# First FFN: block 0 projected in two halves of 256 channels, norm sums taken over channels by TensorE

## The chip, the cores and the metric

The kernel runs on one core of one Trainium2 chip. The metric is device time in microseconds (us) of one execution; the time before is the median of 3 runs. Engines are named as in the profile: PE is TensorE, DVE is VectorE, ACT is ScalarE, POOL is GpSimd, SP is SyncE, which issues the DMAs here.

## The reference, cut to what matters

Two layers act on a residual stream `x` of 256 tokens by 2048 channels, float32. Every sub-layer normalizes, scales and shifts; scale, shift and gate come from one vector `c` through large matrices:

```python
sc = jax.nn.silu(c)
shift_m, scale_m, gate_m, shift_f, scale_f, gate_f = jnp.split(sc @ mod_w[i] + mod_b[i], 6, axis=-1)
h = modulate(rmsnorm(x, norm_mix[i]), shift_m, scale_m)
x = x + gate_m[:, None, :] * pool_mixer(h, pool_w[i], pool_scale[i])     # layer 0; layer 1: attention
h = modulate(rmsnorm(x, norm_ffn[i]), shift_f, scale_f)
x = x + gate_f[:, None, :] * ((silu(h @ w_gate) * (h @ w_up)) @ w_down)
```

`mod_w[i]` is 2048 x 12288: each of the six pieces is 2048 x 2048 float32, 16 MB, and is used once. The change lies where layer 0 passes from its pooling mixer to its FFN.

## The kernel before, in words

**Front.** The first 48 MB of `mod_w[0]` (shift, scale and gate of the mixer) and then the shift and scale of the FFN for channels 0 to 511 (8 MB) are streamed in units of 1 MB into a ring of six buffers (`raw_t`) by DMAs that SP issues in a fixed order. `Strips.use` multiplies a unit by the column of `silu(c)` on PE, 32 rows of the array at a time (L282), or, for seven of the gate's units, on DVE (L265, L267). `Strips.columns` turns the sum into per-channel columns (L287, L291), and `with_bias` adds the bias (L801, L803). The list `units` has 16 + 16 + 16 + 8 units (shift, scale, gate, `block`); `then(n, f)` hangs other work behind unit n: the 64 mixer products (`pool_product`, L864, a group of 8 per call pair), `mix_in` (L874: x + gate * y in the transposed layout `xT`, 16 instructions; L878 and L881: squares on ACT; L882: sums of squares on DVE), `norm_sums` (L892: the rest of the sum over channels on PE, L474, L475, L896), `turn_back` (L903, L904: `xT` back to token rows, which are later written aside to DRAM), `norm_spread` (L908, L909), `hidden_T` (L916: times 1/rms) and `halves_T` (L925 to L927: scale, shift, and the split into a high and a low part). In the front every engine runs in the order in which the code is written.

**FFN.** Each weight unit of 1 MB (512 x 512) is split: `hi` on ACT (L427), `lo` = weight - hi on DVE (L429). `proj_unit` then runs 24 matmuls of 512 columns (hi x high, hi x low, lo x high; four slices of 128 channels; two token halves; L451). `start_ffn` runs blocks j = 0, 1, 2 of 512 channels: in each, twelve units (gate and up of the chunks 0 to 5 of 512 FFN columns). Chunk 0 keeps its four PSUM banks through all blocks; for the others `gather` adds each block's result to a running sum in SBUF: in block 0 a copy on ACT (L616), in later blocks an add on DVE (L618). PSUM has eight banks. I number the units 0 to 35 through the three blocks: units 0 and 1, 12 and 13 belong to chunk 0; unit 20 is the gate unit of chunk 4 in block 1.

**Background.** Beside each block run eight `pump` calls: each loads 1 MB of the shift and scale of the next block's channels and adds it to an accumulator on DVE (`BlockPart.unit`, L311, two instructions of 1024 elements); after eight of them `folded` sums over partitions (L322, L324 on DVE, L328 on PE) and `fin` writes the columns (L765, L766). From the FFN on a scheduler orders the instructions of each engine at build time by priorities; the order is then fixed.

Of the kernel before, what the change touches and what calls it, by code (L numbers as in the profile page):

```python
# [52 lines left out]
C_PAIR = C_SEL + NSTRIP  # L53
C_END = C_PAIR + 2
# [19 lines left out]
def shape_constants():  # L74
# [10 lines left out]
    for i in range(NSTRIP):  # L85
        con[i * STRIP, C_SEL + i] = 1.0
        con[i * STRIP, C_PAIR + i % 2] = 1.0
# [13 lines left out]
def tile_trunk(ctx: ExitStack, tc: tile.TileContext, a: dict, out: bass.AP):  # L101
# [57 lines left out]
    def load_ahead():  # L159
        kt = len(ahead)  # L160
        ahead.append(raw_t([P, 1, NSTRIP, CH]))
        sync.dma_start(ahead[kt].rearrange("p k i n -> p (k i n)"), a["mod_w"][0, kt * P:(kt + 1) * P, :D])
# [80 lines left out]
    class Strips:  # L243
        def __init__(self, i, pair, done, aside=()):
            self.aside, self.acc, self.bank = aside, None, None
            self.n, self.rows, self.done, self.kt = (2, 2, done, 0) if pair else (NSTRIP, 1, done, 0)
            w = a["mod_w"][0][:, i * D:(i + self.rows) * D]
            self.w = w.rearrange("(k p) (i n) -> p k i n", p=P, i=2)[:, :, :, :CH] if pair else                 w.rearrange("(k p) (i n) -> p k i n", p=P, i=NSTRIP)

        def load(self):  # L250
            r = raw_t([P, self.rows, self.n, CH])
            for k in range(self.rows):
                sync.dma_start(r[:, k], self.w[:, self.kt + k])
            return r
# [4 lines left out]
        def use(self, r):  # L259
            last = self.kt + self.rows == KD  # L260
            if self.kt in self.aside:
                s_ = s_col[:, self.kt:self.kt + 1]
                if self.acc is None:
                    self.acc = work.tile([P, 1, NSTRIP, CH], F32, tag="acc", bufs=2, name=nm("acc"))
# [3 lines left out]
            else:  # L268
                self.sum(lambda k: s_strip[:, self.kt + k, :], r, last and self.acc is None)
            if last and self.acc is not None:  # L270
                self.sum(lambda k: one_strip, self.acc, True)
# [4 lines left out]
        def sum(self, weights, r, last):  # L276
# [3 lines left out]
            for m in range(NSTRIP):  # L280
                k, i = m // self.n, m % self.n
                pe.matmul(self.bank[m * STRIP:(m + 1) * STRIP, :], lhsT=weights(k), rhs=r[:, k, i, :], start=first, stop=last)  # L282

        def columns(self):
# [3 lines left out]
            pick = con[:, C_SEL:C_SEL + NSTRIP] if self.rows == 1 else con[:, C_PAIR:C_PAIR + 2]  # L288
            pt = ps_t()
            for b in range(KL):  # L290
                pe.matmul(pt[:, b * self.n:(b + 1) * self.n], lhsT=rows[:, b * P:(b + 1) * P], rhs=pick, start=True,  # L291
                          stop=True)
            return pt[:, :KL * self.n].rearrange("p (b i) -> p i b", i=self.n)


    class BlockPart:
# [3 lines left out]
        def unit(self):  # L300
# [12 lines left out]
            self.kt += 2  # L313
            if self.kt == KD:
# [131 lines left out]
    def proj_unit(banks, t_, hi, lo, first, last, toks=range(NT)):  # L446

        for part in [[tok] for tok in toks] if last else [toks]:
            order = [(w, i, k, tok) for w, i in ((hi, 0), (hi, 1), (lo, 0)) for k in range(KL) for tok in part]
            for n, (w, i, k, tok) in enumerate(order):  # L450
                pe.matmul(banks[tok], lhsT=t_[:, i, k, tok * P:(tok + 1) * P], rhs=w[:, k, :],  # L451
# [145 lines left out]
    class Begun:  # L597
        def __init__(self, w, c, held):
            self.w, self.c, self.held, self.part = w[:, c * CH:(c + 1) * CH], c, held, None

        def block(self, j, t_):
# [5 lines left out]
            if not self.held:  # L607
                pending.append((0, lambda banks=self.banks: self.gather(banks, j)))
                if j == ND - 1:
                    flush()  # L610

# [148 lines left out]
    def sf_block(l, j, cshift, cscale):  # L760
        g0 = V_NF + l * KD + j * KL
        kt = slice(j * KL, (j + 1) * KL)

        def fin(v, rows):
            dve.tensor_copy(cols[rows, cshift, kt], v[:, :KL])  # L765
            dve.scalar_tensor_tensor(out=cols[rows, cscale, kt], in0=v[:, KL:], scalar=1.0,  # L766
                                     in1=vcol[rows, g0:g0 + KL], op0=ALU.add, op1=ALU.mult)

        def done(acc):
            folded(acc.rearrange("p i n -> p (i n)"), 2 * CH, fin)  # L770
# [505 lines left out]
```

## Time and profile before

| | us |
|---|---|
| median of 3 runs | 1956.53 (1955.52 to 1957.05) |
| the profiled execution's own time | 1956.75 |
| its span, first to last instruction | 1954.6 |
| PE busy in the span | 1875.0 |
| DVE busy | 1461.5 |
| ACT busy | 843.9 |
| first FFN matmul (L451) starts at | 176.20 |

The profiled execution is 0.2 us above the median and its span 2.15 us below its own time. Times in rows count from the span's start. A busy share is a mean over stages; the rows of the stage around the change say what ends last there.

### The profile page before, as it was taken

What the parts mean: (1) busy time and instruction counts of PE and PEld (TensorE: products, weight loads), DVE (VectorE), ACT (ScalarE), POOL (GpSimd) and SP (SyncE); (2) the same over time, 40 slices, a digit from 0 to 9 for tenths busy, and PEclk for the clock granted to TensorE, in tenths of its full rate; (3) what the DMA queues carried; (4) which work ended last, traced back from release to release, by engine and by line L of the source; (5) the groups of instructions that cost most, each with busy time, mean ns of one, the idle gap of its engine ahead of it and who ended that gap; (6) DMA issues with size and microseconds to landing.
All of it is one profiled execution on the core that took longest, in us unless ns stands there. A gap on an engine that the chain in (4) does not pass through costs nothing. (4 is left out here: it accounts for less than half of the span.)

```text
span 1954.6 us, 22168 instructions
## 1 busy us (share of the span) xinstructions
PE 1875.0 (96%) x8845; PEld 1519.7 (78%) x8845; DVE 1461.5 (75%) x1312; ACT 843.9 (43%) x915; POOL 30.4 (2%) x32
## 2 busy tenths in 40 slices
PE   6688999999999999998899999999999999999998
PEld 3155888888888888887789987888888888888886
DVE  1147899998788778888999975889986566654556
ACT  3023634444533334325676734544444433343333
POOL 0000000000000000000000000000000000000000
PEclk9788999999999999999999998999999999999999
DMA  9999999989898988997988684989887767665661
GB/s 396 412 415 353 387 329 331 327 302 349 320 333 291 342 306 322 344 345 243 342 312 298 231 282 150 363 295 327 292 295 257 237 219 257 237 212 187 194 219 67
DMA packets 225440, 572.71 MB, mean 293 GB/s; under 512 B 11997, under 2 KB 16421, under 8 KB 203571
## 3 DMA queue, kind: packets, MB, share of 16 engines
q1 hardware_dynamic: 225338, 571.31, 81.7%
q8 instruction: 69, 1.13, 0.2%
q14 instruction: 33, 0.27, 0.0%
HBM read 564.98 MB, written 6.29 MB: 292 GB/s over the span
## 5 line engine op out<-in xcount | busy, mean ns | idle before, releaser
L451 PE MATMUL ps<-hl,act 128*128 128x512 f32 x7008 | 1610.0, 391 | 5.7 <-ACT hl L427 2.1
L451 PEld LDWEIGHTS ps<-hl,act 128*128 128x128 f32 x7008 | 1315.6, 188 | 282.2 <-ACT act L926 3.2
L429 DVE TENSOR_TENSOR hl<-raw,hl 128x2048 fp32r<-128x2048 f32 x296 | 676.6, 2289 | 245.0 <-ACT hl L427 243.7
L427 ACT ACTIVATE hl<-raw 128x2048 fp32r<-128x2048 f32 x296 | 567.1, 1919 | 664.2 <-PE ps L451 587.7
L238 DVE SCALAR_TENSOR_TENSOR acc<-raw,s_col,acc 128x2048 f32<-128x2048 f32 x112 | 262.8, 2347 | 0.6 <-DMA raw<-in_mod_w_dram 0.4
L311 DVE SCALAR_TENSOR_TENSOR acc<-raw,s_col,acc 128x1024 f32<-128x1024 f32 x112 | 143.4, 1281 | 2.0 <-DMA raw<-in_mod_w_dram 0.7
L282 PE MATMUL ps<-raw,front 128*32 128x512 f32 x392 | 64.8, 752 | 27.6 <-DMA raw<-in_mod_w_dram 27.5
L618 DVE TENSOR_TENSOR act<-ps,act 128x512 f32<-128x512 f32 x96 | 64.1, 687 | 10.5 <-PE ps L451 10.2
L282 PEld LDWEIGHTS ps<-raw,front 128*32 128x32 f32 x392 | 9.3, 120 | 60.2 <-DMA raw<-in_mod_w_dram 48.0
L687 DVE TENSOR_TENSOR x<-ps,x 128x512 f32<-128x512 f32 x32 | 22.1, 691 | 33.3 <-PE ps L451 33.2
L470 ACT ACTIVATE junk<-x 128x512 bf16<-128x512 f32 x24 | 15.1, 630 | 59.8 <-DVE x L568 39.7
L652 ACT ACTIVATE act<-ps 128x512 fp32r<-128x512 f32 x44 | 23.6, 593 | 40.0 <-PE ps L649 36.6
L801 DVE TENSOR_TENSOR cols<-ps,front 128x16 f32<-128x16 f32 (+1 forms) x4 | 0.6, 166 | 50.9 <-PE ps L291 50.9
L696 ACT ACTIVATE t2k<-ps 128x512 f32<-128x512 f32 x24 | 14.2, 592 | 56.6 <-PE ps L451 56.6
L1074 PE MATMUL ps<-act,hl 128*128 128x256 f32 x128 | 36.9, 289 | 1.0 <-DVE hl L429 1.0
L1075 PE MATMUL ps<-act,hl 128*128 128x256 f32 x128 | 36.4, 285 | 0.0
L1076 PE MATMUL ps<-act,hl 128*128 128x256 f32 x128 | 35.9, 283 | 0.0
L700 DVE TENSOR_TENSOR t2k<-ps,t2k 128x512 f32<-128x512 f32 x24 | 16.6, 690 | 25.7 <-PE ps L451 25.5
L864 PEld LDWEIGHTS ps<-act,act 128*128 128x128 f32 x128 | 24.1, 194 | 11.4 <-issue 8.4
L864 PE MATMUL ps<-act,act 128*128 128x256 f32 x128 | 31.0, 394 | 0.0
L616 ACT ACTIVATE act<-ps 128x512 f32<-128x512 f32 x32 | 19.0, 596 | 27.2 <-PE ps L451 27.1
L518 ACT ACTIVATE t2k<-ps,cols 128x256 f32<-128x256 f32 x48 | 24.9, 575 | 12.0 <-PE ps L504 11.4
(196 smaller groups left out, 985.1 us busy)
## 6 DMA issues: line engine op xcount, KB each, us to landing
raw<-in_mod_w_dram SPq DMA_DIRECT2D x128, 1024.0 KB, 8.2
raw<-in_ffn_gate_dram SPq DMA_DIRECT2D x88, 1024.0 KB, 6.9
raw<-in_ffn_up_dram SPq DMA_DIRECT2D x88, 1024.0 KB, 5.3
raw<-in_ffn_down_dram SPq DMA_DIRECT2D x88, 1024.0 KB, 5.3
raw<-in_mod_w_dram SPq DMA_DIRECT2D x128, 512.0 KB, 6.3
raw<-in_kv_mod_w_dram SPq DMA_DIRECT2D x32, 1024.0 KB, 7.2
raw<-in_w_o_dram SPq DMA_DIRECT2D x16, 1024.0 KB, 5.7
raw<-in_w_uq_dram SPq DMA_DIRECT2D x8, 768.0 KB, 6.0
```

The costliest lines, as they stand in the source:

```text
L238: dve.scalar_tensor_tensor(out=self.acc, in0=r, scalar=s_col[:, self.kt:self.kt + 1], in1=self.acc, op0=ALU.mult, op1=ALU.add)
L282: pe.matmul(self.bank[m * STRIP:(m + 1) * STRIP, :], lhsT=weights(k), rhs=r[:, k, i, :], start=first, stop=last)
L311: dve.scalar_tensor_tensor(out=self.acc, in0=r[:, k], scalar=s_col[:, self.kt + k:self.kt + k + 1], in1=self.acc, op0=ALU.mult, op1=ALU.add)
L427: hi_ins = act.activation(hi, r, AF.Copy)
L429: lo_ins = dve.tensor_tensor(out=lo, in0=r, in1=hi.bitcast(F32), op=ALU.subtract)
L451: pe.matmul(banks[tok], lhsT=t_[:, i, k, tok * P:(tok + 1) * P], rhs=w[:, k, :], start=first and n < len(part), stop=last and n >= len(ord ...
L518: act.activation(full, pts[k // 2][:, k % 2, :], AF.Identity, scale=scale, bias=bias)
L618: dve.tensor_tensor(out=part, in0=banks[tok], in1=part, op=ALU.add)
L864: pe.matmul(mixed[g][:, n % 2, :], lhsT=wp[g][:, k, ns], rhs=pool_all[g // 2][:, g % 2, k, :], start=k == 0, stop=k == KL - 1)
L1074: pe.matmul(pt[:, h, :], lhsT=wl(h0 + h, k), rhs=t_[:, 0, k, :], start=k == 0, stop=False)
L1075: pe.matmul(pt[:, h, :], lhsT=wh(h0 + h, k), rhs=t_[:, 0, k, :], start=False, stop=False)
L1076: pe.matmul(pt[:, h, :], lhsT=wh(h0 + h, k), rhs=t_[:, 1, k, :], start=False, stop=k == KL - 1)
```

## The change

Channels 0 to 511 of the FFN's input are now made in two halves of 256.

- `units` has four `block` units instead of eight: `Strips(3, True, ...)` takes shift and scale of channels 0 to 255 alone, four DMAs of 256 KB a unit, pieces of 1 KB where there were 2 KB. Channels 256 to 511 come by `HalfPart`, a background part of four units: four DMAs of 256 KB and four DVE instructions of 512 elements each, then `folded`.
- All `mix_in` calls stand behind the last gate unit; the sums of squares over channels are 32 small matmuls (L953 of the new file, `norm_sums(g)`), eight behind each `block` unit, and the DVE sums are gone. The mixer products move one unit forward.
- Block 0 of the FFN runs in `first_halves`: twelve units again, each now 256 channels of gate and up of one chunk (`half_unit`, two DMAs of 512 KB). Units 0 to 5 take channels 0 to 255, units 6 to 11 channels 256 to 511. Outside chunk 0 each unit writes four banks, and `gather` runs once per half: a copy on ACT in the first, an add on DVE in the second and in all later blocks (`later`).
- `FIRST_PUMPS` calls the pump 8 times in the first half and 4 times in the second: the four `HalfPart` units, then the eight units of the next block that stood there before.
- `turn_back` of groups 2 and 3 stands behind units 0 and 1 of the FFN; `hidden_T` and `halves_T` of the second half stand before unit 5.

```diff
-    units = [shift] * KD + [scale] * KD + [gate] * KD + [block] * (KD // 2)
+    units = [shift] * KD + [scale] * KD + [gate] * KD + [block] * (KD // NSTRIP)
...
-            then(n_mix + 1 + 4 * g + q, pool_product, g, q)
-        then(n_block - (g < ND - 1), mix_in, g)
-        then(n_block + 1 + g, turn_back, g)
-    then(n_block + 3, norm_sums)
+            then(min(n_mix + 4 * g + q, n_block - 2), pool_product, g, q)
+        then(n_block - 1, mix_in, g)
+        then(n_block + g, norm_sums, g)
...
+    def norm_sums(g):
+        for k in range(KL):
+            for tok in range(NT):
+                pe.matmul(total[:, tok:tok + 1], lhsT=squares[g, k // 2][:, k % 2, tok * P:(tok + 1) * P],
+                          rhs=ones[:, 0:1], start=g + k + tok == 0, stop=g == ND - 1 and k == KL - 1 and tok == NT - 1)
...
+    class HalfPart:
...
+            r = raw_t([P, KL, 2, CH // 2])
+            for k in range(KL):
+                sync.dma_start(r[:, k], self.w[:, self.kt + k])
+            for k in range(KL):
+                dve.scalar_tensor_tensor(out=self.acc, in0=r[:, k], scalar=s_col[:, self.kt + k:self.kt + k + 1],
+                                         in1=self.acc, op0=ALU.mult, op1=ALU.add)
...
+    FIRST_PUMPS = (2, 1, 1, 1, 1, 2), (2, 2, 0, 0, 0, 0)
+
+    def first_halves(begun, t_):
+        for h in range(2):
+            for c in begun:
+                if h == 1 and c == BEGUN - 1:
+                    after = halves_T(1, ahead)
+                hi, lo = first_unit if h + c == 0 else split(*half_unit(c, h))
+                if h == 0 and c == BEGUN - 1:
+                    halves_T(0, hidden_T(0, 1), 1, t_)
+                for i in range(2):
+                    begun[c][i].half(h, t_, hi[:, i], lo[:, i])
+                if h == 0 and c < 2:
+                    turn_back(2 + c)
+                if h == 1 and c == BEGUN - 3:
+                    ahead = hidden_T(1)
+                pump(FIRST_PUMPS[h][c])
...
+    push(sf_block(0, 0, C_SF0, C_AF0, True), KD // KL)
```

The order of instructions moves at three places. In the rows below `L429` before is `L450` after (the `lo` of a unit; `hl_1013` and `hl_1078` are the low parts of units 2 and 3), and `L618` is `L649` (a gather).

First, DVE in block 0 of the FFN, just ahead of a `lo`. Before, around unit 2:

```order
L311 SCALAR_TENSOR_TENSOR acc_963<-raw_1003,s_col,acc_963 128x1024
L429 TENSOR_TENSOR hl_976<-raw_973,hl_975 128x2048
L311 SCALAR_TENSOR_TENSOR acc_963<-raw_1003,s_col,acc_963 128x1024
L916 TENSOR_TENSOR t2k_1715<-x,krT 128x256 x2
L916 TENSOR_TENSOR t2k_2187<-x,krT 128x256 x2
L916 TENSOR_TENSOR t2k_2190<-x,krT 128x256
L311 SCALAR_TENSOR_TENSOR acc_963<-raw_1040,s_col,acc_963 128x1024
L429 TENSOR_TENSOR hl_1013<-raw_1010,hl_1012 128x2048
```

After, the end of the stretch between the `lo` of units 2 and 3, in which eleven of the sixteen `HalfPart` instructions (L332) stand:

```order
L332 SCALAR_TENSOR_TENSOR acc_946<-raw_1062,s_col,acc_946 128x512
L980 TENSOR_TENSOR t2k_2292<-x,krT 128x256
L332 SCALAR_TENSOR_TENSOR acc_946<-raw_1062,s_col,acc_946 128x512
L980 TENSOR_TENSOR t2k_2295<-x,krT 128x256
L343 STREAM_TRANSPOSE raw_1071<-acc_946 128x512
L980 TENSOR_TENSOR t2k_2295<-x,krT 128x256
L345 TENSOR_REDUCE acc_946<-raw_1071 128x16
L311 SCALAR_TENSOR_TENSOR acc_1113<-raw_1116,s_col,acc_1113 128x1024
L450 TENSOR_TENSOR hl_1078<-raw_1074,hl_1077 128x2048
```

What moved: the sixteen `HalfPart` adds and their fold, which did not exist, stand between the `lo` of units 1 and 3, and eight copies of `turn_back` between those of units 0 and 3.

Second, DVE at the end of block 0, from the fold of the next block's columns on. Before (units 8 to 11; no gather stands here):

```order
L324 TENSOR_REDUCE acc_963<-raw_1246 128x32
L429 TENSOR_TENSOR hl_1254<-raw_1251,hl_1253 128x2048
L429 TENSOR_TENSOR hl_1288<-raw_1285,hl_1287 128x2048
L429 TENSOR_TENSOR hl_1322<-raw_1319,hl_1321 128x2048
L429 TENSOR_TENSOR hl_1379<-raw_1376,hl_1378 128x2048
```

After (units 8 to 10, with the gathers of units 7 and 8):

```order
L345 TENSOR_REDUCE acc_1113<-raw_1323 128x32
L450 TENSOR_TENSOR hl_1330<-raw_1326,hl_1329 128x2048
L649 TENSOR_TENSOR gate_901<-ps_1285,gate_901 128x512
L649 TENSOR_TENSOR gate_901<-ps_1286,gate_901 128x512
L450 TENSOR_TENSOR hl_1369<-raw_1365,hl_1368 128x2048
L649 TENSOR_TENSOR gate_901<-ps_1299,gate_901 128x512
L450 TENSOR_TENSOR hl_1414<-raw_1410,hl_1413 128x2048
L649 TENSOR_TENSOR gate_901<-ps_1300,gate_901 128x512
```

What moved: twenty adds from PSUM stand on DVE between the `lo` of unit 8 and that of unit 14.

Third, PE around the end of the gate (`acc_533` is the part summed on DVE; `ps_708` and `ps_758` are the last group of mixer products). Before:

```order
L282 MATMUL ps_537<-raw_712,front 32x512 x4
L282 MATMUL ps_537<-acc_533,front 32x512 x4
L291 MATMUL ps_724<-con,t2k_722 128x4 x4
L864 MATMUL ps_758<-act_120,act_502 128x256 x4
L282 MATMUL ps_766<-raw_763,front 32x512 x4
L864 MATMUL ps_758<-act_120,act_502 128x256 x4
```

After:

```order
L932 MATMUL ps_686<-act_120,act_502 128x256 x4
L283 MATMUL ps_542<-raw_702,front 32x512 x4
L932 MATMUL ps_708<-act_120,act_502 128x256 x8
L283 MATMUL ps_542<-raw_721,front 32x512 x4
L283 MATMUL ps_542<-acc_533,front 32x512 x4
L292 MATMUL ps_733<-con,t2k_731 128x4 x4
```

And at the end of the front after, on PE (`raw_827` is the last `block` unit; `t2k_758` to `t2k_770` are the last squares):

```order
L953 MATMUL ps_719<-ones,t2k_758 128x1 x4
L953 MATMUL ps_719<-ones,t2k_762 128x1 x4
L283 MATMUL ps_777<-raw_827,front 32x512 x4
L292 MATMUL ps_838<-con,t2k_836 128x1 x4
L953 MATMUL ps_719<-ones,t2k_766 128x1 x4
L953 MATMUL ps_719<-ones,t2k_770 128x1 x4
L971 MATMUL ps_719<-t2k_718,ones 128x256
```

What moved: the last group of eight products stands ahead of the gate's columns, and the last eight sums of squares stand behind the columns of the `block` units.

More of the change, by code (lines that the diff above doesn't have):

```diff
@@ L280, in sum @@
             for m in range(NSTRIP):
[L281 to L282 removed]
+                pe.matmul(self.bank[m * STRIP:(m + 1) * STRIP, :], lhsT=weights(m), rhs=r[:, m], start=first, stop=last)
         def columns(self):
@@ L779, in start_ffn @@
         with tc.issue_after(mod_ins[0].ins):
-            for j in range(ND - 1):
+            if l == 0:
+                hT.append(first_halves(begun, first))
+            for j in range(l == 0, ND - 1):
                 if l == 0 and j == 1:
@@ L972, in tile_trunk @@
                 f(*args)
-        first = halves_T(0, first[0])
+        norm_finish()
+        hi, lo = first_unit = hl_t(shape), hl_t(shape)
+        act.activation(hi, r, AF.Copy)
+        norm_spread()
+        first = halves_T(0, hidden_T(0, 0))
+        dve.tensor_tensor(out=lo, in0=r, in1=hi.bitcast(F32), op=ALU.subtract)
+        for g in range(2):
+            turn_back(g)
     aside[0] = dram.tile([P, NT, D], F32, name=nm("aside"))
+    push(sf_block(0, 0, C_SF0, C_AF0, True), KD // KL)
     for j in range(1, ND):
```

145 lines of the change are left out of this document (83 added, 62 removed).

## The prediction

> **What bounds the kernel.** I read the page's busy parts first, then windows around the change, then the timeline of DVE and PE there.
>
> ```profile
> span 1954.6 us, 22168 instructions
> PE 1875.0 (96%) x8845; PEld 1519.7 (78%) x8845; DVE 1461.5 (75%) x1312; ACT 843.9 (43%) x915; POOL 30.4 (2%) x32
> L451 PE MATMUL ps<-hl,act 128*128 128x512 f32 x7008 | 1610.0, 391 | 5.7 <-ACT hl L427 2.1
> ```
>
> PE is busy for 96% of the span, and its large matmuls wait 5.7 us in all: once the FFN has begun, PE sets the end. Whatever makes PE start earlier or stand still later moves the end by as much. The windows show who could make it stand:
>
> ```profile
> 150.00:200.00 50.00, 42.79 (x214) 27.56 (x214) 41.28 (x67) 20.43 (x26) 2.18 (x3) 0.90 0.99 353
> 200.00:220.00 20.00, 20.00 (x89) 16.54 (x89) 19.82 (x14) 10.21 (x11) 0.00 (x0) 1.00 1.02 390
> 220.00:240.00 20.00, 19.61 (x86) 15.62 (x85) 14.96 (x17) 15.99 (x20) 0.95 (x1) 1.00 1.05 386
> 260.00:300.00 40.00, 40.00 (x178) 33.12 (x177) 38.31 (x33) 13.81 (x8) 0.00 (x0) 1.00 0.91 315
> 300.00:350.00 50.00, 50.00 (x223) 41.42 (x222) 48.55 (x51) 21.40 (x18) 1.82 (x1) 1.00 0.93 320
> 169.07:290.85 121.78, 118.17 (x523) 93.68 (x516) 107.13 (x104) 60.53 (x60) 2.43 (x3) 0.98 0.98 352
> ```
>
> Columns: stretch, length, busy us of PE, PEld, DVE, ACT, POOL, PE's clock, DMA share, GB/s. DVE is at 96 to 99% in 200:220, 260:300 and 300:350, the same stretches in which PE is full. DVE has almost no room beside blocks 0 to 2 of the FFN; its 75% of the span hides that. How close it is:
>
> ```profile
> 1339.27 59.85 PE ps L451 x264
> ...
> 169.07 2.28 DVE L429 TENSOR_TENSOR hl<-raw,hl 128x2048 fp32r<-128x2048 f32 x1
> ...
> 221.31 1.92 ACT L427 ACTIVATE hl<-raw 128x2048 fp32r<-128x2048 f32 x1 [3.00 <-DMA raw<-in_ffn_gate_dram]
> ...
> 267.92 0.69 DVE L618 TENSOR_TENSOR gate<-ps,gate 128x512 f32<-128x512 f32 x1 [0.84 <-PE ps L451]
> ...
> 273.84 0.68 DVE L618 TENSOR_TENSOR act<-ps,act 128x512 f32<-128x512 f32 x1
> 274.44 1.27 DVE L311 SCALAR_TENSOR_TENSOR acc<-raw,s_col,acc 128x1024 f32<-128x1024 f32 x1
> 275.64 2.28 DVE L429 TENSOR_TENSOR hl<-raw,hl 128x2048 fp32r<-128x2048 f32 x1
> 277.84 0.68 DVE L618 TENSOR_TENSOR act<-ps,act 128x512 f32<-128x512 f32 x1
> ...
> 288.57 2.28 DVE L429 TENSOR_TENSOR hl<-raw,hl 128x2048 fp32r<-128x2048 f32 x1
> ```
>
> A matmul takes 59.85/264 = 0.227 us, a unit of 24 takes 5.44. The gather at 267.92 waited for PE to end unit 15. Unit 20 begins four units later, at 267.9 + 21.8 = 289.7, and needs its `lo` eight matmuls on, at 291.5. That `lo` (288.57 + 2.28) is ready at 290.85: 0.6 us to spare. From start to start a gather costs DVE 0.60 us (273.84 to 274.44), an add of 1024 elements 1.20, a `lo` 2.20. DVE takes its instructions in a fixed order, so unit 20's `lo` comes after everything listed ahead of it. I use it as the gauge: later by x there, and PE's end is later by x - 0.6.
>
> **The sum on DVE.** From the `lo` of unit 0 (169.07) to that of unit 20 before, DVE works 107.1 of 121.8 us and idles 14.7. Added in that stretch, by the new order:
> - Twenty gathers (block 0's second half, four outside-chunk banks a unit) at 0.60: 12.0.
> - Sixteen `HalfPart` adds of 512 elements. No row has that width. Between 0.41 (256 wide, row 148.72 below) and 1.20 (1024 wide) I take the line between them, 0.67: 10.7; the ends are 6.6 and 19.2.
> - The fold of 512 elements, half of the two rows below, 1.2, and eight small writes at 0.16, 1.3.
>
> ```profile
> L322 DVE STREAM_TRANSPOSE raw<-acc 128x1024 f32<-128x1024 f32 x2 | 2.5, 1248 | 0.1
> L324 DVE TENSOR_REDUCE acc<-raw 128x32 f32<-128x1024 f32 x2 | 2.4, 1220 | 0.1
> L765 DVE COPY cols<-ps 32x4 f32<-32x4 f32 x4 | 0.6, 158 | 0.9 <-PE ps L328 0.9
> ```
>
> - Eight copies of `turn_back`, ahead of 169.07 before: 0.60 each as a gather, 4.8.
> - Less: `hidden_T` and `halves_T` of two slices and three small writes of columns now lie ahead of the stretch (rows 171.37, 177.13 and 174.64 below: 0.36, 0.4 and 0.2 each): -2.0.
>
> Sum 28.0, so 135.1 us of DVE work where 121.8 us went by. Even with no idle time left, the stretch is 13.3 us longer than before. Unless it begins 13 us sooner, PE loses.
>
> **When it begins.** The front before:
>
> ```profile
> 133.75 1.06 PE L282 MATMUL ps<-raw,front 128*32 128x512 f32 x8
> ...
> 134.74 3.72 PE L864 MATMUL ps<-act,act 128*128 128x256 f32 x16
> ...
> 145.45 1.04 PE L282 MATMUL ps<-acc,front 128*32 128x512 f32 x8
> ...
> 148.72 2.46 DVE L874 SCALAR_TENSOR_TENSOR x<-act,front,x 128x256 f32<-128x256 f32 x6
> 149.70 0.63 ACT L878 ACTIVATE t2k<-x 128x512 f32<-128x512 f32 x1 [2.54 <-DVE x L874]
> ...
> 152.55 0.69 DVE L882 TENSOR_TENSOR t2k<-t2k,t2k 128x512 f32<-128x512 f32 x1
> ...
> 153.95 1.09 PE L903 MATMUL ps<-con,x 128*128 128x128 f32 x8
> ...
> 163.06 1.60 PE L892 MATMUL ps<-ones,t2k 128*128 128x1 f32 x8 [3.98 <-DVE t2k L882]
> ...
> 165.68 0.48 DVE L896 TENSOR_SCALAR t2k<-con,sm 128x128 f32<-128x128 f32 x2 [0.82 <-POOL sm L475]
> ...
> 170.22 0.70 PE L908 MATMUL ps<-t2k,ones 128*128 128x256 f32 x2
> ...
> 171.37 1.43 DVE L916 TENSOR_TENSOR t2k<-x,krT 128x256 f32<-128x256 f32 x4
> 172.90 0.60 ACT L287 ACTIVATE t2k<-ps 128x512 f32<-128x512 f32 x1 [1.56 <-PE ps L282]
> ...
> 174.64 0.23 DVE L801 TENSOR_TENSOR cols<-ps,front 128x4 f32<-128x4 f32 x2 [1.83 <-PE ps L291]
> ...
> 175.10 0.60 ACT L925 ACTIVATE t2k<-t2k,cols 128x256 f32<-128x256 f32 x1 [1.61 <-DVE cols L803]
> ...
> 176.20 0.74 PE L451 MATMUL ps<-hl,act 128*128 128x512 f32 x2 [1.60 <-ACT act L926]
> ...
> 177.13 0.43 DVE L927 TENSOR_TENSOR act<-t2k,act 128x256 fp32r<-128x256 f32 x1 [0.52 <-ACT act L926]
> ```
>
> The gate's last strip ends at 146.49 (145.45 + 1.04). Strips and products alternate on PE without a gap before that (133.75 + 1.06 against 134.74), so the group that now stands ahead of the gate's columns adds its 3.72: 150.2. If PE's gaps swallow it, nothing; I take the row. To `mix_in` 2.2 as before: 152.4. Sixteen at 0.41: 159.0. The last square takes 0.63 (149.70): 159.7. ACT, in order, copies the strips of `block` only now, and the four column matmuls behind it stand ahead of the last eight norm sums: 172.90 to 174.64, 1.7, so 161.4. Eight norm sums, 1.60 for four at PE's low clock, half at full: between 1.6 and 3.2, I take 2.4: 163.8. Then 1.5 (164.66 to 166.16), 1.15 (170.22 to 171.37), 0.4 for the first slice, and 1.1 to the first FFN matmul (175.10 to 176.20): 168.0, 8.2 us sooner than before. The `lo` of unit 0 stands behind the second slice's split: 175.10 to 177.56, 2.46, so it begins at 169.3. That is where it stood before. The seven DVE sums that go (0.69 each at 152.55, 4.8), the four strips units less (1.06 each on PE) and `turn_back` moved behind have brought PE's start forward, not DVE's.
>
> **The sum.** 169.3 + 135.1 = 304.4, against 291.5: +12.9. DVE will not be without any idle time: gathers wait for PE (0.84 at 267.92), and the aside write is issued only behind `turn_back`'s copies, with the next weights queued behind it on SP. I allow 2: +15. The profiled execution, 1956.75, becomes 1971.8; it lies 0.2 above the median, so 1971.5. PE's own addition inside the FFN, `turn_back` of two groups (four times four transposes at 1.09, row 153.95: 4.4), is covered by PE's waiting for `lo`; without that cover it would be paid. After unit 20 the blocks are as before and DVE as full (97% in 300:350), so nothing is won back, and PE, at 5.7 us of waits in all, has no later wait that could absorb it.
>
> Ends: without the group 3.7 less, norm sums 0.8 less, adds of 0.41 4.1 less, no idle 2 less: +4.4. With adds of 1.20 8.5 more: +23.5, norm sums 0.8 more.
>
> **DMA.** The eight MB of `block` and `HalfPart` come in 1 KB pieces, four requests of 256 KB a unit instead of two.
>
> ```profile
> 130.00:135.00 5.00, 4.93 (x29) 3.33 (x26) 2.35 (x1) 0.60 (x1) 0.00 (x0) 1.00 1.01 421
> 155.00:160.00 5.00, 4.08 (x33) 1.99 (x32) 5.00 (x12) 2.41 (x5) 0.00 (x0) 1.00 1.05 387
> ```
>
> 8 KB pieces moved at 421 GB/s, 2 KB pieces in requests of 512 KB at 387. The same loss per piece again twice over (a piece costs 9 ns beside its bytes) gives some 350 at 1 KB: 8.4 MB take 24.0 us for 21.7. Spread over a block in which DVE is the later one, I count it at nothing; if DVE were not late, the 2.3 would show, since the cast at 221.31 waited 3.00 us for its weights. If a request took the same time at half the size, the rate would be 194 GB/s: the upper end.
>
> The Trainium skill speaks harder against the change: its page "DMA: Bandwidth & Descriptors", section "Measured (HBM→SBUF, 128 partitions, SWDGE, issued from GpSimd)", says to batch DMAs to 1 MiB or more for 75% of peak, and puts 64 KB at 138 GB/s and 1 MB at 341. By that page 256 KB would lie between these two, at some 200 GB/s (an estimate from it), and the sum would gain what rival 4 gives. The trace does not bear it out for 512 KB, which moved at 387.
>
> **Rivals.**
> 1. DVE's load is absorbed and the earlier start carries through: first matmul 8.2 sooner, less 4.4 of transposes: 1956.5 - 3.8 = 1952.7; without the late group, 1949. It decides at unit 20's `lo`: DVE must end it by 287.7, 118 us after 169.3, with 135 us of work listed. For it speaks only that DVE idles 14.7 before. Against it, the order. Chance 0.08.
> 2. DMA holds unit 8 as it did at 221.31, and DVE fits: the start's gain is eaten by the same transfer plus 2.3, 1956 to 1959. Chance 0.04.
> 3. PSUM banks. Outside chunk 0 a unit writes all four free banks, and each waits for the gather of the unit before; in the second half those gathers stand on DVE behind two or three `lo`s. PE and DVE then wait for each other in turn: units 8 to 11 at a `lo` and four gathers plus a wait each, 8 us more than the sum: 1979. Chance 0.13.
> 4. Requests of 256 KB run at half the rate (194 GB/s): 8.4 MB take 43 us instead of 22, and the half that lies ahead of the FFN delays DVE's start by 10.8 if nothing covers it: 1982. The 421 against 387 above speak against so steep a fall. Chance 0.05.
>
> **How the numbers follow.** My forecast, slower by DVE's work, has 0.70, with a range of its own of 1963 to 1979. Slower in all: 0.70 + 0.13 + 0.05 = 0.88. About 0.2% (3.9 us) is what a measurement of this kernel can tell from no change. Rival 2 is mostly within it: same 0.04; faster 0.08. The range from 1961 to 1981 holds the forecast's and rival 3's cases, and leaves out rivals 1, 2 and 4 (0.17) and the outer ends.
>
> **What would show it.** Right: DVE at 97% or more from 175 to 300; PE with waits of over 5 us for `lo` at unit 3 and again at units 6 to 8; unit 20's `lo` ending near 305; the first FFN matmul near 168; PE from block 2 on as before. Wrong: a `lo` of unit 3 that comes before 190, or DVE idle in block 0 of more than 10 us (then DMA or banks), or the gate's columns at 148 (then the start was mis-sized).

## The result, and the profile after

The changed kernel takes 1988.88 us (median of 4 runs, 1987.85 to 1989.57), the kernel before 1956.03 in the same series (1955.02 to 1957.05): 1.0167 times as long, 95% interval 1.015 to 1.0185. The forecast was 1971.5, slower, with a range of 1961 to 1981. The sign came true; the loss is 32.9 us instead of 15.

The page of the changed kernel, its first lines and its large matmuls:

```profile
span 1987.6 us, 22310 instructions
PE 1891.1 (95%) x8871; PEld 1536.5 (77%) x8871; DVE 1482.1 (75%) x1351; ACT 842.8 (42%) x915; POOL 30.9 (2%) x33
L473 PE MATMUL ps<-hl,act 128*128 128x512 f32 x7008 | 1615.2, 392 | 25.3 <-ACT act L647 9.9
```

The large matmuls wait 25.3 us instead of 5.7 and are busy 5.2 us longer in all (1615.2 against 1610.0). Shares of the span hardly moved, so the page alone does not tell where the time went. A window from the first FFN matmul to the end does (columns as in the prediction; the clock is PE's granted clock as a share of full speed). First the kernel before, then the changed one:

```profile
176.20:1954.64 1778.44, 1749.37 (x8128) 1459.00 (x8128) 1405.54 (x1200) 802.89 (x837) 25.98 (x19) 0.99 0.80 282
```

```profile
182.56:1987.55 1804.99, 1756.19 (x8149) 1463.41 (x8147) 1437.92 (x1256) 801.14 (x836) 26.91 (x20) 0.99 0.79 279
```

The end is the start of the FFN, plus what PE does from there, plus what it stands still. Start: 182.56 against 176.20, 6.4 later. Busy: 1756.19 against 1749.37, 6.8 more. Idle: 48.8 against 29.1, 19.7 more. Together 32.9, the whole difference. The later table uses this account. Most of the 6.8 are the 5.2 of the large matmuls, some of which run at half speed behind a long wait: the 48 that begin at 213.40 below take 12.66 us, where 48 at 0.227 take 10.9, and the clock is 0.50 in 213.40:216.40. The transposes of two groups of `turn_back`, 1.03 us each, are in it too.

The same stretches of the changed kernel as the prediction showed of before, and last the stretch from `lo` of unit 0 to `lo` of unit 20:

```profile
150.00:200.00 50.00, 44.05 (x217) 33.48 (x208) 25.22 (x48) 16.24 (x22) 2.18 (x3) 0.73 0.54 175
200.00:220.00 20.00, 10.06 (x37) 7.62 (x36) 19.14 (x29) 7.35 (x9) 0.53 (x1) 0.74 0.97 351
220.00:240.00 20.00, 17.52 (x77) 13.85 (x75) 18.61 (x22) 10.86 (x16) 0.96 (x1) 1.00 1.05 386
260.00:300.00 40.00, 40.00 (x178) 32.97 (x179) 38.80 (x46) 16.74 (x15) 0.95 (x1) 1.00 0.83 293
300.00:350.00 50.00, 49.22 (x218) 40.43 (x217) 49.29 (x53) 22.11 (x18) 1.81 (x1) 1.00 0.94 325
182.94:324.22 141.28, 118.69 (x508) 94.80 (x506) 135.11 (x151) 57.11 (x54) 2.44 (x3) 0.94 0.86 305
```

Three things stand out. In 150:200 PE is busy for 44 us, but its clock is 0.73 (0.90 before), and the DMA engines move 175 GB/s instead of 353. In 200:220 PE stands half the time while DVE is full. And in the last row DVE works 135.11 us, which is the forecast's 135.1, in 141.28.

The front on PE, from the timeline (start, length; the last bracket is the idle time before and what ended it):

```profile
152.62 1.06 PE L283 MATMUL ps<-raw,front 128*32 128x512 f32 x8
154.81 3.36 PE L953 MATMUL ps<-ones,t2k 128*128 128x1 f32 x16 [1.12 <-ACT t2k L947]
158.10 1.93 PE L283 MATMUL ps<-raw,front 128*32 128x512 f32 x8
159.96 3.57 PE L953 MATMUL ps<-ones,t2k 128*128 128x1 f32 x16
...
171.62 1.86 PE L292 MATMUL ps<-con,t2k 128*128 128x1 f32 x8 [0.85 <-ACT t2k L288]
173.34 3.55 PE L953 MATMUL ps<-ones,t2k 128*128 128x1 f32 x16
```

L953 is the small matmul of `norm_sums`; the 8 matmuls of a group leave 16 records. From 155 on everything runs at half speed (clock 0.50 in 160:170, shown with e2 below): the strips take 1.93 instead of 1.06, a group 3.36 to 3.57. PE takes its instructions in order, so the strips, the columns behind them and the last group all wait for the groups ahead. The sums end at 176.89 (173.34 + 3.55).

Block 0 of the FFN, from the timeline of PE (the waits at units 3, 7 and 8) and that of DVE (the `lo` of units 0, 2, 3 and, in block 1, 20):

```profile
213.40 12.66 PE L473 MATMUL ps<-hl,act 128*128 128x512 f32 x48 [9.94 <-ACT act L647]
...
241.36 1.88 PE L473 MATMUL ps<-hl,act 128*128 128x512 f32 x7 [2.31 <-ACT hl L448]
...
253.75 6.60 PE L473 MATMUL ps<-hl,act 128*128 128x512 f32 x19 [5.23 <-DVE gate L649]
```

```profile
182.94 2.29 DVE L1040 TENSOR_TENSOR hl<-raw,hl 128x2048 fp32r<-128x2048 f32 x1
...
196.84 2.28 DVE L450 TENSOR_TENSOR hl<-raw,hl 128x2048 fp32r<-128x2048 f32 x1
...
213.50 2.28 DVE L450 TENSOR_TENSOR hl<-raw,hl 128x2048 fp32r<-128x2048 f32 x1
...
321.93 2.28 DVE L450 TENSOR_TENSOR hl<-raw,hl 128x2048 fp32r<-128x2048 f32 x1
```

Units 2 and 3 have their `lo` 16.7 us apart, where PE needs 5.44 us a unit. Unit 20's `lo` ends at 324.21; before it was 290.85. That is 33.4 later, less the 0.6 of slack: 32.8. The gauge of the prediction holds.

What the DMA queue on SP waited for between 165 and 270 us (total, times, longest):

```profile
SPq L330 <- DVE hl L1040: 13.5, 1, 13.5
SPq L819 <- DVE act L967: 13.3, 2, 12.5
```

L330 loads a `HalfPart` piece; its buffer is freed by the `lo` of unit 0. L819 is the aside write; it needs the last copies of `turn_back`. Behind each, all later weights wait. PE's longest wait in the changed kernel comes from this. ACT, in order, stands 14.74 us for the weights of unit 3, and its copies of unit 2's banks (L647) stand behind that cast:

```profile
210.95 1.91 ACT L448 ACTIVATE hl<-raw 128x2048 fp32r<-128x2048 f32 x1 [14.74 <-DMA raw<-in_ffn_up_dram]
212.77 2.04 ACT L647 ACTIVATE act<-ps 128x512 f32<-128x512 f32 x4
```

DVE comes to unit 3's `lo` at the same time, 213.50. Of PE's waits at large matmuls between 165 and 340 us only 3.6 us end with a `lo`; 9.9 end with ACT's copies, 5.2 with a gather on DVE and 3.8 with a cast.

### The profile page after: what moved, and what is told of

Read it like the earlier page. It is cut to its first block, busy times and chain, and to the rows that moved or that the text cites. A ratio compares the mean times of both kernels' runs of the same rounds, so it can differ in the third digit from the quotient of the medians.

```text
span 1987.6 us, 22310 instructions
## 1 busy us (share of the span) xinstructions
PE 1891.1 (95%) x8871; PEld 1536.5 (77%) x8871; DVE 1482.1 (75%) x1351; ACT 842.8 (42%) x915; POOL 30.9 (2%) x33
## 5 line engine op out<-in xcount | busy, mean ns | idle before, releaser
L473 PE MATMUL ps<-hl,act 128*128 128x512 f32 x7008 | 1615.2, 392 | 25.3 <-ACT act L647 9.9
L450 DVE TENSOR_TENSOR hl<-raw,hl 128x2048 fp32r<-128x2048 f32 x295 | 673.9, 2288 | 240.2 <-ACT hl L448 235.6
L649 DVE TENSOR_TENSOR act<-ps,act 128x512 f32<-128x512 f32 x112 | 74.3, 685 | 11.8 <-PE ps L473 11.3
L283 PEld LDWEIGHTS ps<-raw,front 128*32 128x32 f32 x360 | 8.7, 123 | 57.2 <-DMA raw<-in_mod_w_dram 46.1
L526 PE MATMUL ps<-con,t2k 128*128 128x128 f32 x112 | 17.7, 310 | 11.1 <-DVE t2k L514 8.0
```

Source lines behind the costliest of these rows:

```text
L450: lo_ins = dve.tensor_tensor(out=lo, in0=r, in1=hi.bitcast(F32), op=ALU.subtract)
L473: pe.matmul(banks[tok], lhsT=t_[:, i, k0 + k, tok * P:(tok + 1) * P], rhs=w[:, k, :], start=first and n < len(part), stop=last and n >= le ...
L649: dve.tensor_tensor(out=part, in0=banks[tok], in1=part, op=ALU.add)
```

## The experiments

Each edit is against the changed kernel unless said otherwise. "Idle" is PE's idle time from the first FFN matmul on. Kernels e3, e6, e8, e9, e10, e12 and e13 do not compute the whole result; what each leaves out or does twice is said with it.

| run | time, us | first FFN matmul | idle |
|---|---|---|---|
| before | 1956.03 | 176.20 | 29.1 |
| changed | 1988.88 | 182.56 | 48.8 |
| e1 sums on DVE | 1979.75 | 173.71 | 47.2 |
| e2 before, sums on PE | 1954.92 | 174.91 | 27.4 |
| v1 e2, transposes later | 1961.56 | 181.33 | 29.6 |
| e7 no gap | 1986.24 | 178.89 | 48.7 |
| e11 transposes between | 1989.86 | 188.90 | 43.6 |
| e15 e11 and no gap | 1980.61 | 180.38 | 44.0 |
| e3 gathers off DVE | 1984.68 | 183.11 | 45.8 |
| e8 gathers twice | 2004.32 | 182.95 | 60.7 |
| e4 aside later | 1989.83 | 182.28 | 45.4 |
| e6 e1, e3 and e4 | 1980.46 | 173.58 | 46.9 |
| e9 small adds | 1988.23 | 182.70 | 47.2 |
| e10 e9 and e3 | 1985.77 | 182.24 | 44.9 |
| e12 e9 and e4 | 1980.65 | 182.95 | 40.8 |
| e13 e9, e3 and e4 | 1978.94 | 182.37 | 38.8 |
| e16 first `lo` early, e4 | 1985.94 | 182.48 | 46.1 |

The runs of e7, e10 and e11 spread over 4 to 8 us (1982.34 to 1986.44, 1981.63 to 1986.48, 1982.96 to 1990.93); why is open, and differences of 3 us and less from the changed kernel, here medians of four runs, are weak evidence.

### The front: what the norm sums cost

**e1**: the sums as before.

```diff
-            squares[g, h2] = sq
+            late.append(lambda sq=sq: dve.tensor_tensor(out=squares[0], in0=squares[0], in1=sq, op=ALU.add))
...
-        then(n_block + g, norm_sums, g)
+    then(n_block + 3, norm_sums)
```

> The changed kernel with the norm sums as they were before: VectorE adds the squares (seven adds of 0.69 us) and TensorE sums them in 4 small matmuls of 0.40 us behind the last strips, where the change has 32 of about 0.45 us between the strips. Theory A (the 32 small matmuls, in TensorE's order between the strips and at its half clock, hold the front up by what the trace shows beyond the forecast, 13 us): first FFN matmul near 169 us instead of 182.6, `lo` of unit 0 near 170, end 1976 us, 12 to 14 less than the changed kernel. Rival B (VectorE's and the transfers' work in block 0 of the FFN sets unit 20, and a sooner start is eaten there): 1986 to 1989. Rival C (the empty DMA queue behind the aside write is the loss): about 1987, since that queue stays as it is.

1979.75 us (1.0125 of before, 1.0108 to 1.0142): 9.1 less than the changed kernel. The first FFN matmul comes 8.9 sooner, and DVE's stretch has not changed by it:

```profile
173.91:314.94 141.03, 121.47 (x509) 96.60 (x508) 135.15 (x151) 56.91 (x54) 2.44 (x3) 0.93 0.86 306
```

So a sooner front is carried through to the end; rivals B and C fall for this part. Theory A's size was somewhat high: 9, not 12 to 14. Since the adds are back between the instructions of `mix_in`, the last square ends later again, at 162.8 instead of 160.3.

**e2**: the kernel before, with only the sums moved to PE (the seven adds on DVE go; `...` stands for that part).

```diff
-    then(n_block + 3, norm_sums)
+    for g in range(ND):
+        then(n_block + g, norm_sums, g)
...
```

> The kernel before with one part of the change alone: the norm sums over channels as 32 small matmuls on TensorE, eight behind each of the four last strips units, and without the seven adds of squares on VectorE. Theory A (they lengthen the front): three groups of 8 at 3.4 to 3.6 us stand ahead of the last one, and 8 small matmuls stand where 4 did; less the seven adds that VectorE is spared; 8 to 13 us slower than before, 1964 to 1969. Rivals B and C (the front's length is not the cause): 1955 to 1959.

1954.92 us (0.9996, 0.9987 to 1.0005): no difference, against theory A as it stood. The windows of e2 and of the changed kernel show why:

```profile
160.00:170.00 10.00, 10.00 (x84) 6.67 (x86) 5.62 (x10) 2.25 (x2) 0.70 (x1) 1.00 1.04 381
```

```profile
160.00:170.00 10.00, 10.00 (x52) 7.33 (x48) 0.00 (x0) 0.32 (x1) 0.00 (x0) 0.50 0.93 306
```

PE is full in both, but at clock 1.00 in e2 and 0.50 in the changed kernel. In e2 a group takes 1.84 us:

```profile
160.44 1.84 PE L885 MATMUL ps<-ones,t2k 128*128 128x1 f32 x16
```

So the number of small matmuls does not set their time. In e2 each group has eight transposes of `turn_back` (1.09 us) and strips beside it; v1 takes the transposes away from there.

**v1**: e2 with those transposes three strips units later. PE's instructions are the same, in another order.

```diff
-        then(n_block + 1 + g, turn_back, g)
+        then(n_block + 4 + g, turn_back, g)
```

> The kernel before with the norm sums on TensorE and, besides, the 32 transposes that turn x back and their eight copies three strips units later, so that norm sums and strips come sooner on TensorE. If the front is TensorE's: first FFN matmul up to 4 us sooner than 176.2, end 1952 to 1955. If the strips' weights (the DMA engines move 380 GB/s there, share 1.0) or VectorE at unit 20 bound it: 1954 to 1957.

Slower: 1961.56 us (1.003 of before, 1.0018 to 1.0041), 6.6 more than e2, and the first FFN matmul 6.4 later. Neither expectation had it. The same window:

```profile
160.00:170.00 10.00, 10.00 (x48) 7.22 (x48) 0.36 (x2) 1.91 (x1) 0.70 (x1) 0.50 0.98 354
```

PE has no idle moment from 153.6 to 177.9, and yet its clock fell to 0.50, where strips and small matmuls alone alternate. It came back at 172, beside transposes (strips at 1.07 us again).

**e7**: five matmuls of 128x256 more in the changed kernel's gap of 1.12 us.

```diff
+        if g == 0:
+            for _ in range(5):
+                pe.matmul(total[:, T:], lhsT=ones, rhs=con[:, :T], start=True, stop=True)
```

> The changed kernel with five matmuls of 128x256 more (their result is not read) ahead of the first norm sums, where TensorE stood still for 1.12 us at 153.7 and its clock went from 1.0 to 0.5. Theory E (the front is long because the clock falls in that gap and the sparse small matmuls don't bring it back): clock 1.0 to 170, a group of norm sums in 1.84 us as in the kernel before with the sums on TensorE, instead of 3.5; first FFN matmul 172 to 173, end 1978 to 1980. Rival F (the small matmuls alone, without a gap, let the clock fall): clock 0.5 again from the first or second group on, first FFN matmul 182 to 184, end 1988 to 1991. Rival B (only the number of matmuls counts): as F.

```profile
156.00 1.84 PE L956 MATMUL ps<-ones,t2k 128*128 128x1 f32 x16
157.77 1.07 PE L283 MATMUL ps<-raw,front 128*32 128x512 f32 x8
158.76 1.95 PE L956 MATMUL ps<-ones,t2k 128*128 128x1 f32 x16
160.64 1.06 PE L283 MATMUL ps<-raw,front 128*32 128x512 f32 x8
161.63 3.48 PE L956 MATMUL ps<-ones,t2k 128*128 128x1 f32 x16
```

Between the theories: full speed for two groups, then half, as in v1. First FFN matmul 3.7 sooner, time 1986.24 (1982.34 to 1986.44), 2.6 less.

**e11**: the transposes between the groups, as before; **e15**: that and the five matmuls of e7.

```diff
         then(n_block + g, norm_sums, g)
+        then(n_block + g, turn_back, g)
...
-                if h == 0 and c < 2:
-                    turn_back(2 + c)
...
-        for g in range(2):
-            turn_back(g)
```

> The changed kernel with the 32 transposes that turn x back between the groups of norm sums, one group of 8 behind each, where they stood before; their eight copies (4.8 us of VectorE) come out of the FFN's first units. Theory E+F (strips and small matmuls alone let TensorE's clock fall to 0.5, as 1.06 us strips and 1.84 us groups did in the kernel before when the transposes were moved out from between them; 1.09 us of transposes a group keep it at 1.0): a group of norm sums 1.84 us, clock 1.0 to 170, first FFN matmul 174 to 177 in spite of 4.4 us more work ahead of it, end 1973 to 1980. Rival B (the time of a small matmul does not depend on what stands around it): groups of 3.5 us, first FFN matmul 185 to 188, end 1984 to 1990.

> The changed kernel with the transposes between the groups of norm sums and five matmuls of 128x256 in TensorE's gap of 1.12 us ahead of the first group. With the first edit alone the clock fell in that gap and stayed at 0.5 (groups of 3.58 us, first FFN matmul at 188.9); with the second alone it held for two groups and then fell. Theory E (a gap starts it, sparse work keeps it; without either it stays at 1.0): four groups of 1.84 us, first FFN matmul 176 to 178, end 1975 to 1980 with the aside write where it was. Rival F (any group of small matmuls lets it fall here): 186 to 189, end 1985 to 1990.

e11 missed theory E+F and came out as its rival B had it: 1989.86, groups of 3.58 us and the transposes at half speed too. The clock had fallen behind the gap, and this mixture did not bring it back. That the time does not depend on the neighbours, as rival B has it, e15 refutes. It closes the gap and has 1980.61, 9.3 less, with the first FFN matmul 8.5 sooner:

```profile
160.00:170.00 10.00, 9.15 (x78) 6.71 (x75) 4.15 (x8) 2.70 (x4) 0.00 (x0) 1.00 1.03 336
```

Clock 1.00 to 170; only the last group, behind a wait of 0.85 us for the strips' copy, ran at half (3.39 us), so the start is 180.4 and not 176 to 178. Gap and sparse work each let the clock fall: in v1 it fell without the gap, in e11 in spite of the transposes, and in e15, without either, it held for three groups. The five matmuls close the gap and are dense work themselves; which of the two counts was not separated.

### Block 0 of the FFN: what holds PE

**e3**: the second half's gathers as copies on ACT; the first half's result is not added.

```diff
-                pending.append((0, lambda banks=self.banks: self.gather(banks, h)))
+                pending.append((0, lambda banks=self.banks: self.gather(banks, 0)))
```

> The changed kernel with the 20 gathers of block 0's second half as copies on ScalarE; it leaves out the adding of the first half's result there. That takes 20 times 0.60 us = 12.0 us from VectorE inside the stretch from the `lo` of unit 0 to that of unit 20 (141.3 us). Theory A (VectorE's listed work sets that stretch, but the transfers behind the aside write and TensorE's own work lie close under it): 4 to 8 us less than the changed kernel, 1981 to 1985. Rival D (VectorE alone sets the stretch): 12 less, 1977. Rival C (the transfers behind the aside write set it): 0 to 2 less, 1987 to 1989.

**e8**: each of these gathers twice, on DVE (that half's result is added twice).

```diff
-                pending.append((0, lambda banks=self.banks: self.gather(banks, h)))
+                pending.append((0, lambda banks=self.banks: self.gather(banks, h, 1 + h)))
...
-            for tok in range(NT):
+            for tok in [tok for tok in range(NT) for _ in range(times)]:
```

> The changed kernel with each of the 20 gathers of block 0's second half done twice on VectorE (so that half's result is added twice): 20 times 0.60 us = 12.0 us more on VectorE between unit 0's `lo` and unit 20's. Theory A (VectorE's 135.1 us of work set that stretch, with 6.2 idle): the idle time is of waits elsewhere and can take little; end 8 to 13 us later, 1997 to 2002. Rival C (the transfers behind the aside write set it, VectorE stands just under them): 2 to 6 later, 1991 to 1995.

Twelve us less on DVE gave 4.2 less (1984.68, theory A's range), twelve more gave 15.4 more (2004.32, above both ranges). The stretches of e3 and e8:

```profile
183.32:318.36 135.04, 117.02 (x504) 93.86 (x503) 123.16 (x131) 66.39 (x74) 2.43 (x3) 0.95 0.89 321
```

```profile
183.17:337.67 154.50, 121.62 (x509) 96.07 (x508) 147.16 (x171) 57.14 (x54) 2.43 (x3) 0.92 0.78 276
```

Upwards DVE sets the stretch, and the doubled gathers hold PE's banks longer too: the wait for one at unit 8 is 8.54 us in e8, for 5.23. Downwards another bound is close: DVE idles 11.9 us in e3, 6.2 in the changed kernel.

**e4**: the aside write behind block 0's weights.

```diff
-                    for tok in range(NT):
-                        sync.dma_start(aside[0][:, tok], back[tok])
+                    with tc.issue_after(w_load[0].ins):
+                        for tok in range(NT):
+                            sync.dma_start(aside[0][:, tok], back[tok])
```

> The changed kernel with the aside write issued behind the last weights of block 0, so that no weights of block 0 stand behind it in SP's queue; its work is the same. In the changed kernel the DMA engines move 99 and 6 GB/s in 180:200 and the weights of unit 3 come 14.7 us late to ScalarE. Theory A (VectorE's work is the stretch, the queue costs what the stretch has beyond the listed work): 3 to 5 us less, 1984 to 1986. Rival C (that empty queue is the main loss): 13 to 15 less, 1974 to 1976. Rival B (whatever starts sooner is caught at unit 20 by VectorE): no difference, 1987 to 1990.

No gain: 1989.83, as rival B had it. PE's waits in 165:340 (total, times, longest) show the one at unit 3 as long as it was, now ended by `lo` rather than by ACT:

```profile
PE ps L473 <- DVE hl L450: 16.5, 6, 10.3
```

**e6**: e1, e3 and e4 together.

> The changed kernel with three edits at once: norm sums on VectorE as before, the aside write behind block 0's weights, and the 20 gathers of the second half as copies on ScalarE (it leaves out the adding of the first half's result there). The first edit alone gave 1979.75 us, the second alone nothing, the third alone 4.2 less. Theory D (VectorE's work alone sets the stretch from unit 0's `lo` to unit 20's, and only the write's queue kept the third edit from its 12): stretch 129, end 1967 to 1969. Theory A (weights that come at the full rate of the DMA engines lie some 6 us under VectorE's work): stretch 133 to 136, end 1972 to 1976.

Missed by both: 1980.46, no more than e1 alone. In e6 PE waits 10.55 us for unit 3's `lo`, and from 261 to 312 us it is full:

```profile
207.38 12.19 PE L473 MATMUL ps<-hl,act 128*128 128x512 f32 x42 [10.55 <-DVE hl L450]
...
261.60 51.06 PE L473 MATMUL ps<-hl,act 128*128 128x512 f32 x224 [0.65 <-ACT hl L448]
```

The gathers stand at units 7 to 11. PE had lost most of its time before, at unit 3, ahead of whose `lo` all sixteen half-width adds stand in DVE's list, and could not win it back.

**e9**: those adds over 32 of their 512 elements (the rest of that shift and scale is left out; the loads stay). **e10**: e9 and e3.

```diff
-                dve.scalar_tensor_tensor(out=self.acc, in0=r[:, k], ...
+                dve.scalar_tensor_tensor(out=self.acc[:, :, :16], in0=r[:, k, :, :16], ...
```

> The changed kernel with each of the 16 half-width adds over 32 of its 512 elements (the rest of the block's shift and scale is left out; the loads stay). By 0.66 us from start to start now and about 0.16 for so small a one, VectorE loses 8.0 us, 5.5 of them ahead of unit 3's `lo`. Theory G (TensorE loses its time at units 1 to 9, where VectorE's list is longer than TensorE's, and is full from 261 us on): `lo` of unit 3 6 to 8 us sooner than 213.5, TensorE's wait there 2 to 4 us instead of 9.9, end 5 to 8 us sooner, 1981 to 1984. Theory D (only the sum up to unit 20 counts, wherever it stands): the same 4.2 for 12 as the copies on ScalarE gave, here 2 to 3: 1986 to 1987. Rival C (transfers bind in block 0): 1987 to 1989.

> Both reliefs at once: the half-width adds over 32 of 512 elements, and the 20 gathers of the second half as copies on ScalarE (the first half's result and most of the shift and scale are left out). Theory G: 8 us of the early list and 12 of the late one; alone each is held by the other, together they give more than their sum of 6 to 8 and 4.2: end 1971 to 1976. Theory C (the transfers of block 0, at the full rate from 205 to 260 us, bind next): no more than the first alone, 1980 to 1984.

Both missed theory G: 1988.23 and 1985.77, within 0.7 and 3.1 of the changed kernel, though DVE has 7.6 us less to do in e9. e9 lies where its rival C (the transfers bind) had it, e10 above both its ranges. In e9 DVE idles instead:

```profile
200.00:210.00 10.00, 3.48 (x16) 2.54 (x14) 4.57 (x16) 0.00 (x1) 0.53 (x1) 0.84 0.99 352
```

```profile
211.34 1.28 DVE L311 SCALAR_TENSOR_TENSOR acc<-raw,s_col,acc 128x1024 f32<-128x1024 f32 x1 [6.70 <-DMA raw<-in_mod_w_dram]
```

Now the weights are late. In e9 the aside write is issued at 199.45, and the first weights behind it at 200.43.

**e12**: e9 and e4. **e13**: e9, e4 and e3.

> Two edits that gave nothing alone: the half-width adds over 32 of 512 elements (most of that shift and scale is left out), and the aside write issued behind block 0's weights. Theory H (two bounds lie side by side in block 0: VectorE's list, and the weights, whose transfers stand still from 180 to 200 us behind two waiting requests in SP's queue; each relief alone runs into the other): together 5 to 9 us sooner than the changed kernel, 1980 to 1984, TensorE's wait at unit 3 gone to below 4 us. Rival I (something else, TensorE's own order, bounds): 1986 to 1989, as each alone.

> The same with the 20 gathers of the second half as copies on ScalarE as well (the first half's result and most of the shift and scale are left out): 20 us off VectorE and the aside write out of the way. Theory H: VectorE's stretch falls below TensorE's; what is left is the queue's first wait (13.5 us for unit 0's `lo`) and 4.4 us of transposes: 1972 to 1978. Rival I: 1982 to 1986, as without the third.

e12 takes 1980.65 us, 8.2 less than the changed kernel and in theory H's range, out of two edits that alone gave nothing that can be told from noise (0.7 less and 1.0 more). Its stretch, with DVE's work as in e9:

```profile
183.16:317.60 134.44, 121.30 (x509) 97.23 (x508) 127.40 (x151) 57.20 (x54) 2.43 (x3) 0.95 0.90 320
```

The wait at unit 3 is 3.25 us. So two bounds of the same height lay there, DVE's list and the weights behind the aside write, and each hid the other. e13 with 1978.94 gives 1.7 more, less than expected. What is left of its waits is nearly all for `lo`: 11.9 us in seven waits, six of them in block 0.

**e16**: e4, and unit 0's cast and `lo` ahead of the last strips unit; it computes the whole result (`...` stands for e4's edit and for the lines that go at the old place).

```diff
...
+            if n == n_block + 3:
+                hi, lo = first_unit = hl_t(shape), hl_t(shape)
+                act.activation(hi, r, AF.Copy)
+                dve.tensor_tensor(out=lo, in0=r, in1=hi.bitcast(F32), op=ALU.subtract)
...
```

> The changed kernel, complete, with unit 0's cast and `lo` ahead of the last strips unit, where ScalarE and VectorE have nothing to do (160 to 171 us), and the aside write behind block 0's weights. SP's two long waits (13.5 us for that `lo` to free a buffer, 12.5 for the last copies of x) both go; VectorE's list loses 2.2 us. Theory H: the transfers start some 15 to 20 us sooner, VectorE's list (133 us) remains the bound: lo of unit 20 2 to 6 us sooner, end 1983 to 1987. Theory C (the transfers' late start is the main loss): 10 to 15 us sooner, 1974 to 1979. Rival I: 1987 to 1990.

1985.94, 2.9 less, as theory H had it. SP's two old waits are gone, but at one load it now waits 18.8 us for DVE. So far as this shows, the transfers' late start alone is not the main loss; DVE's list is, as soon as they are in time: PE waits 8.80 us for unit 3's `lo`.

No version beat both kernels: e2 is the fastest, and not to be told from before.

## Why the prediction was right and wrong

It read a right bound and the right gauge, and so the sign: DVE has no room in blocks 0 to 2, and what makes `lo` of unit 20 later makes the end later. A second bound of the same height beside DVE's list is not in its sum. By its own terms:

- **DVE's added work, 28.0 us: right.** 135.11 us were measured for 135.1, with the half-width add from start to start at 0.66 for my interpolated 0.67.
- **The gate's group, 3.72, and `mix_in`: right.** The last square ended at 160.3 for 159.7.
- **"Eight norm sums ... I take 2.4": the step that failed.** Only the last group was priced; that 24 more stand in PE's order ahead of the last strips, columns and group was not counted at all, and the half clock was kept for one group. Measured: four groups of 3.36 to 3.57, and the strips between them at 1.93, so the sums end at 176.9 instead of 163.8. What follows them took 5.7 us, for 4.2. `lo` of unit 0 began at 182.9 instead of 169.3: 13.6 of the 17.4 that were missing. e1 shows 9 of these to be the place of the sums; e2, v1, e7 and e15 show the clock behind them. For the other 4 to 5 us of the start no run separates the DVE adds that e1 brings back from work that is still at half clock.
- **"I allow 2" of idle time: too small.** 6.2 were measured, 4.2 more. Beside the 13.6 this is the rest of the error: 13.6 + 4.2 = 17.8, for 17.4.
- **"Four times four transposes at 1.09 ... 4.4": a misreading.** The row of 1.09 us is a whole group's eight transposes, so two groups are 2.2; 1.03 each were measured. The sum did not use the 4.4, rival 1's time did.
- **SP's queue: named, and priced too low.** The prediction saw the aside write behind `turn_back`'s copies. The weights behind it are a second bound as high as DVE's list (e12), and a first wait of 13.5 us for unit 0's `lo` was not seen.
- **Rivals.** DVE did not absorb its work (1). The bank mechanism (3) shows as it was described once: 5.23 us at 253.75, for a gather that stands behind unit 8's `lo`, where 8 had been priced. The 9.94 at unit 3 is a wait for banks too, but behind ACT's late cast. Small requests (4) were no matter: 220:240 moved 386 GB/s, and the 1 KB pieces of the strips in 155:160 moved 346 at a DMA share of 1.08, for my estimate of 350. Rival 2's late weights are real, but beside a full DVE.
- **The signs.** The first FFN matmul came at 182.56 and not near 168, the end of unit 20's `lo` at 324.2 and not near 305: wrong, by the front. PE's wait at unit 3 was 9.94, for over 5: right in size, but it ended with ACT's copies behind late weights and not with `lo`; only with the weights in time (e4) did `lo` end it, after 10.3. At units 6 and 7 single waits were 1.1 to 2.3, for over 5: wrong; at unit 8 it was 5.23, for a bank and not for `lo`. DVE worked 95.6% of the stretch (135.11 of 141.28), for 97. From 350 us on PE is idle 26.2 us, before 27.8: as forecast, next to nothing is won back or lost later.

What stays open is the last 10 us of idle time in e13 (38.8 against 29.1). Its longest wait, 3.4 us, is for a `lo` with four `BlockPart` adds just ahead of it on DVE; spreading those over other units was not tried.

## What to carry to other kernels

Price every moved instruction at each place of an in-order queue where it now stands, at the clock that its neighbours leave there: in the kernel before, the same 32 small matmuls cost nothing between transposes (e2), and 6.6 us once the transposes stood elsewhere (v1). Where relieving the engine that looks full gives nothing, relieve it together with what fed it, before giving up the theory: two bounds of one height hide each other. And write the result as start, busy and idle of the bounding engine, since these three numbers said at once how many causes to look for.

## What the runs showed of the hardware

PE's clock fell to 0.5 while PE was busy throughout (v1, 10.00 of 10.00 us in 160:170). In the changed kernel it fell after a gap of only 1.12 us, and it stayed low for 26 us in which small matmuls and strips made up most of the work (0.50 in 156:182). A matmul of 128x1 then takes 0.45 us (3.57 / 8) instead of 0.23 (1.84 / 8 in e2). Ahead of large matmuls the changed kernel shows another limit: behind waits of 1.52 and 2.31 us the clock was 1.00 (233.30:236.00 and 241.30:243.30), behind 5.23 and 9.94 us it was 0.50 for the next 3 us (253.75:256.75 and 213.40:216.40).

The Trainium skill's page "TensorE: Matmul & The Clock Gate", in its section "Why this matters for your kernels", asks for no idle gaps of more than about 3 us between bursts of matmuls. The four waits ahead of large matmuls agree with it. Ahead of sparse work a gap of 1.12 us was enough, and in v1 none was needed: e2 and v1 differ only in whether transposes stand between the groups. By the Trainium skill's same page, section "What's actually happening", a monitor sets the clock from how busy PE has lately been. These rows agree with that only if strips and small matmuls count there as less than busy, which no run here shows directly.
